# Batched matmul minus a tensor: rings of slots and one listed order of larger transfers in place of pools of four-tile buffers

## The chip, the cores and the metric

One core of a Trainium2 chip, the other cores idle. The metric is the device time of one execution in microseconds. The profile of one execution is taken beside it; its span is 1.7 to 2.2 us shorter than the time of the run. All runs told of here were in the fast state.

## The reference

```python
def setup_inputs():
    batch, m, k, n = 16, 512, 1024, 768     # all float32
    ...
def reference(x, weight, sub_value):
    return (np.matmul(x, weight) - sub_value).astype(np.float32)
```

x is 33.6 MB, the weights 3.1, sub_value and the output 25.2 each: 87.0 MB cross between HBM and SBUF.

## The kernel before

The 8192 rows are 64 tiles of 128. Of each block of 1024 rows, a partition holds eight consecutive ones, so tile j of the block is row j of each partition, and several tiles side by side are one contiguous run per partition. A tile's way: x is loaded, ScalarE casts it to f16 (`cast`), TensorE transposes it and ScalarE copies it back from PSUM (for 14 of the tiles, in pairs, VectorE transposes instead), TensorE runs 16 matmuls, VectorE subtracts sub in place (`finish`), and the result is stored. Everything is kept in program order on each engine, and the transfers are all issued from one queue, SyncE's.

```python
G = 4                       # tiles in a buffer and in a transfer
XA, SA, OA = 3, 2, 2        # groups that x and sub run ahead, and that a store comes behind
...
    x_pool = ctx.enter_context(tc.tile_pool(name="x_pool", bufs=4))
    so_pool = ctx.enter_context(tc.tile_pool(name="so_pool", bufs=7))
...
    for mi in range(HEAD, n_mt):
        g, j = divmod(mi, G)
        if j == 0 or mi == HEAD:
            if g + XA < n_g:
                load_x((g + XA) * G, G)
            if g + SA < n_g:
                load_sub((g + SA) * G, G)
            if g >= OA:
                store((g - OA) * G, G)
        ...                 # matmuls of tile mi, transposes of tile mi + 2, casts ahead
        finish(mi)
        ...
    for g in range(n_g - OA, n_g - 1):
        store(g * G, G)
    store(n_mt - G, G - 2)
    store(n_mt - 2, 1)
    store(n_mt - 1, 1)
```

## Time and profile before

| | before |
|---|---|
| time, median (all runs beside the changed kernel's) | 213.07 us (212.68 to 213.75, 4 runs) |
| span of the profiled run | 211.1 us |
| transfers, descriptors on the queue | 65, 9360 |
| share of the transfers / TensorE | 98.2% / 94% |
| last subtraction ends | 204.96 us |
| from there to the end of the span | 6.1 us |

Two resources are nearly full, so shares alone don't say which sets the end. The last two rows do: they split the end into TensorE's path and what follows it. The prediction below shows the lines. One more row matters, and the prediction didn't use it. It is from the list of transfer issues of the kernel before (count, size, median us from issue to landing), the two last stores of one tile each:

```profile
out_dram<-so_tile SPq DMA_DIRECT2D x2, 384.0 KB, 6.0
```

### The profile page before, as it was taken

What the parts mean: (1) busy time and instruction counts of PE and PEld (TensorE: products, weight loads), DVE (VectorE), ACT (ScalarE), POOL (GpSimd) and SP (SyncE); (2) the same over time, 40 slices, a digit from 0 to 9 for tenths busy, and PEclk for the clock granted to TensorE, in tenths of its full rate; (3) what the DMA queues carried; (4) which work ended last, traced back from release to release, by engine and by line L of the source; (5) the groups of instructions that cost most, each with busy time, mean ns of one, the idle gap of its engine ahead of it and who ended that gap; (6) DMA issues with size and microseconds to landing.
All of it is one profiled execution on the core that took longest, in us unless ns stands there. A gap on an engine that the chain in (4) does not pass through costs nothing.

```text
span 211.1 us, 3028 instructions
## 1 busy us (share of the span) xinstructions
PE 198.0 (94%) x1249; PEld 129.7 (61%) x1249; DVE 114.0 (54%) x186; ACT 112.7 (53%) x115; POOL 0.7 (0%) x6
## 2 busy tenths in 40 slices
PE   7899799999999999999989999997999999999960
PEld 3455567666666676676656567664656666667630
DVE  0343313152697299389519939941993993142330
ACT  3636666757852847465086555509646453556300
POOL 1000000000000000000000000000000000000000
PEclk9999999999999999999999999999999999999995
DMA  6999999999999999999999999999999999999994
GB/s 217 422 413 406 415 418 446 418 425 440 414 429 420 433 426 423 435 421 435 424 422 432 424 434 422 435 420 432 425 429 435 414 428 416 434 412 433 428 409 162
DMA packets 9374, 87.23 MB, mean 413 GB/s; under 512 B 1040, under 2 KB 1040, under 8 KB 3728
## 3 DMA queue, kind: packets, MB, share of 16 engines
q1 hardware_dynamic: 9360, 87.04, 98.2%
q8 instruction: 10, 0.16, 0.3%
q14 instruction: 4, 0.03, 0.0%
HBM read 61.87 MB, written 25.17 MB: 412 GB/s over the span
## 4 chain that ended last, share of the span: by engine, by line
DMA 49%; PE 33%; ACT 9%; DVE 3%; SPq 2%; issue 1%; ACTq 0%
DMA x_tile<-in_x_dram 49%; PE psum_o L149 28%; PE psum_t L116 5%; ACT x_tile L108 4%; ACT xt_tile L123 3%; ACT x16p_tile L105 2%; DVE xtp_tile L137 2%; DVE so_tile L160 1%; SPq L79 1%; SPq L87 1%; ACTq L105 0%
## 5 line engine op out<-in xcount | busy, mean ns | idle before, releaser
L149 PE MATMUL psum_o<-w_sb,xt_tile 128*128 128x384 f16 x800 | 145.9, 326 | 1.7 <-ACT xt_tile L123 1.7
L149 PEld LDWEIGHTS <-xt_tile 128*128 128x128 f16 x800 | 78.1, 98 | 42.0 <-ACT xt_tile L123 2.8
L160 DVE TENSOR_TENSOR so_tile<-psum_o,so_tile 128x768 f32<-128x768 f32 x64 | 60.7, 956 | 57.3 <-PE psum_o L149 34.1
L123 ACT COPY xt_tile<-psum_t 128x1024 f16<-128x1024 f16 x50 | 50.6, 1012 | 58.7 <-PE psum_t L116 58.0
L137 DVE STREAM_TRANSPOSE xtp_tile<-x16p_tile 32x256 f32<-32x256 f32 x112 | 48.8, 436 | 22.4 <-ACT x16p_tile L105 20.6
L108 ACT CAST x_tile<-x_tile 128x1024 f16<-128x1024 f32 x50 | 51.7, 1049 | 7.3 <-DMA x_tile<-in_x_dram 7.3
L116 PE MATMUL psum_t<-ident,x_tile 128*128 128x128 f32 x200 | 52.4, 274 | 2.3 <-ACT x_tile L108 1.9
L149 PE MATMUL psum_o<-w_sb,xtp_tile 128*128 128x384 f16 x224 | 42.9, 326 | 0.6 <-DVE xtp_tile L137 0.6
L116 PEld LDWEIGHTS psum_t<-ident,x_tile 128*128 128x128 f32 x200 | 27.5, 141 | 16.5 <-ACT x_tile L108 4.7
L149 PEld LDWEIGHTS <-xtp_tile 128*128 128x128 f16 x224 | 21.7, 98 | 10.9 <-DVE xtp_tile L137 1.4
L105 ACT CAST x16p_tile<-x_tile 128x1024 f16<-128x1024 f32 x14 | 14.6, 1046 | 20.5 <-DMA x_tile<-in_x_dram 20.5
L81 DVE CAST w_sb<-w_stage 128x768 f16<-128x768 f32 x8 | 4.1, 556 | 10.4 <-DMA w_stage<-in_weight_dram 10.4
L177 PE MATMUL psum_o<-idle_x,idle_w 128*128 128x512 f16 x25 | 7.7, 461 | 1.3 <-DVE idle_x L172 1.3
L177 PEld LDWEIGHTS <-idle_w 128*128 128x128 f16 x25 | 2.9, 116 | 4.5 <-issue 2.4
L108 ACT ACT_TABLE_LOAD x1 | 1.3, 1283 | 0.7 <-PEq L261 0.7
L171 DVE MEMSET idle_w<- 128x64 uint32 x1 | 0.1, 112 | 0.8 <-PEq L261 0.8
masks.py:199 POOL TENSOR_SCALAR_AFFINE_SELECT ident<-ident 128x128 f32<-128x128 f32 x1 | 0.3, 292 | 0.1
L172 DVE MEMSET idle_x<- 128x256 uint32 x1 | 0.3, 272 | 0.0
masks.py:197 POOL MEMSET ident<- 128x128 f32 x1 | 0.2, 205 | 0.3 <-POOLq L261 0.3
L261 POOL MEMSET const-uint8-127<- 128x1 uint8 x1 | 0.1, 102 | 0.0
L261 POOL MEMSET const-bfloat16-1.0<- 128x1 bf16 x1 | 0.1, 101 | 0.0
L261 POOL MEMSET const-float32-0.0<- 128x1 f32 x1 | 0.1, 98 | 0.2 <-issue 0.2
(1 smaller groups left out, 0.1 us busy)
## 6 DMA issues: line engine op xcount, KB each, us to landing
x_tile<-in_x_dram SPq DMA_DIRECT2D x13, 2048.0 KB, 30.9
out_dram<-so_tile SPq DMA_DIRECT2D x15, 1536.0 KB, 31.7
so_tile<-in_sub_value_dram SPq DMA_DIRECT2D x14, 1536.0 KB, 33.0
x_tile<-in_x_dram SPq DMA_DIRECT2D x8, 512.0 KB, 10.6
w_stage<-in_weight_dram SPq DMA_DIRECT2D x4, 768.0 KB, 8.5
x_tile<-in_x_dram SPq DMA_DIRECT2D x2, 1024.0 KB, 13.0
so_tile<-in_sub_value_dram SPq DMA_DIRECT2D x4, 384.0 KB, 11.7
so_tile<-in_sub_value_dram SPq DMA_DIRECT2D x2, 768.0 KB, 13.6
```

The source lines that it names most:

```text
L79: keep(nc.sync.dma_start(out=st, in_=w_c[c]))
L81: keep(nc.vector.tensor_copy(out=w_sb[:, c, r], in_=st[:, r]))
L87: keep(nc.sync.dma_start(out=x_t[g][:, j : j + n], in_=rows(x_s, mi, n)))
L105: keep(nc.scalar.copy(out=x16_t["pair", first][:, mi - first], in_=x_t[g][:, j]))
L108: keep(nc.scalar.copy(out=x16_t[mi], in_=x_t[g][:, j]))
L116: keep(nc.tensor.transpose(ps_t[mi].bitcast(F32)[:, c * P : (c + 1) * P], x16_t[mi].bitcast(F32)[:, c * P : (c + 1) * P], ident,))
L123: keep(nc.scalar.copy(out=xt_t[mi], in_=ps_t.pop(mi)))
L137: keep(nc.vector.transpose(xt[b * Q : (b + 1) * Q, :, a * Q : (a + 1) * Q], x16[a * Q : (a + 1) * Q, :, b * Q : (b + 1) * Q],))
L149: keep(nc.tensor.matmul(po_t[mi][:, h, :NS], xt_t[mi][:, 2 * P * c + r : 2 * P * (c + 1) : 2], w_sb[:, c, r, h * NS : (h + 1) * NS], start ...
L160: keep(nc.vector.tensor_tensor(out=o, in0=po_t.pop(mi)[:, :, :NS], in1=o, op=mybir.AluOpType.subtract))
L177: keep(nc.tensor.matmul(idle_o[:, 0], idle_w, idle_x, start=True, stop=True))
L261: nc = _bacc.Bacc("TRN2", target_bir_lowering=False, num_devices=1)
```

## The change

The pools become two rings, 16 slots for x and 32 shared by sub and the output (the weights pass through eight of these first). Transfers stand in one list, up to eight tiles each, and each is issued as soon as the program has recorded what it needs: a cast for the slot of x, a subtraction for a store, an earlier store for the slot of sub. x runs ahead early; stores wait until late.

```diff
-G = 4
-XA, SA, OA = 3, 2, 2
+NX, NSO = 16, 32
-HEAD_TRANSFERS = [('x', 0, 1), ('w', 0, 0), ('x', 1, 1), ... ('x', 3, 1), ('s', 0, 1), ('x', 4, 1), ('s', 1, 1), ... ('s', 6, 2)]
+TRANSFERS = [
+    ('x', 0, 1), ('w', 0, 1), ('x', 1, 1), ('w', 1, 1), ('x', 2, 1), ('w', 2, 1),
+    ('w', 3, 1), ('x', 3, 2), ('s', 0, 1), ('x', 5, 3), ('s', 1, 3), ('x', 8, 3),
+    ('s', 4, 4), ('x', 11, 5), ('s', 8, 8), ('x', 16, 8), ('x', 24, 3), ('s', 16, 8),
+    ('x', 27, 5), ('o', 0, 8), ('s', 24, 8), ('x', 32, 8), ('s', 32, 8), ('o', 8, 8),
+    ('x', 40, 8), ('s', 40, 8), ('x', 48, 8), ('o', 16, 8), ('o', 24, 8), ('s', 48, 8),
+    ('x', 56, 8), ('s', 56, 8), ('o', 32, 8), ('o', 40, 8), ('o', 48, 8), ('o', 56, 4),
+    ('o', 60, 2), ('o', 62, 1), ('o', 63, 1),
+]
...
+    x_ring = x_pool.tile([P, NX, K], F32)
+    so_ring = so_pool.tile([P, NSO, N], F32)
+    def issue():                # called after each cast and each finish
+        while todo:
+            kind, at, n = todo[0]
...                             # return if what it needs is not yet recorded
+            here = ring[:, at % size : at % size + n]
+            there = view[at // S][:, at % S : at % S + n]
...
-            if g + XA < n_g:
-                load_x((g + XA) * G, G)
...                             # the loads and stores of the main loop go
```

More of the change, by code (lines that the diff above doesn't have):

```diff
@@ L22 @@
 ON_DVE = frozenset(range(18, 60, 6))
-HEAD_TRANSFERS = [('x', 0, 1), ('w', 0, 0), ('x', 1, 1), ('w', 1, 0), ('x', 2, 1), ('w', 2, 0), ('w', 3, 0), ('x', 3, 1), ('s', 0, 1), ('x', 4, 1), ('s', 1, 1), ('x', 5, 1), ('s', 2, 1), ('x', 6, 1), ('s', 3, 1), ('x', 7, 1), ('x', 8, 2), ('s', 4, 2), ('x', 10, 2), ('s', 6, 2)]
+TRANSFERS = [
[7 rows of a table added]
+]
 @with_exitstack
@@ L44 @@
     n_mt = M_TOT // P
-    n_g = n_mt // G
     NS = N // 2
@@ L59 @@
     w_pool = ctx.enter_context(tc.tile_pool(name="w_pool", bufs=1))
-    x_pool = ctx.enter_context(tc.tile_pool(name="x_pool", bufs=4))
+    x_pool = ctx.enter_context(tc.tile_pool(name="x_pool", bufs=1))
     x16_pool = ctx.enter_context(tc.tile_pool(name="x16_pool", bufs=CA + 2))
@@ L64 @@
     xtp_pool = ctx.enter_context(tc.tile_pool(name="xtp_pool", bufs=2))
-    so_pool = ctx.enter_context(tc.tile_pool(name="so_pool", bufs=7))
+    so_pool = ctx.enter_context(tc.tile_pool(name="so_pool", bufs=1))
     psum_t_pool = ctx.enter_context(tc.tile_pool(name="psum_t", bufs=2, space=bass.MemoryType.PSUM))
@@ L73 @@
     w_sb = w_pool.tile([P, n_c, 2, N], F16)
-    x_t, so_t, x16_t, xt_t, ps_t, po_t = {}, {}, {}, {}, {}, {}
-    def load_w(c):
-        st = so_pool.tile([P, 2, N], F32, name="w_stage", tag="so_tile")
-        keep(nc.sync.dma_start(out=st, in_=w_c[c]))
-        for r in range(2):
-            keep(nc.vector.tensor_copy(out=w_sb[:, c, r], in_=st[:, r]))
-    def load_x(mi, n):
-        g, j = divmod(mi, G)
-        if j == 0:
-            x_t[g] = x_pool.tile([P, G, K], F32, name="x_tile")
-        keep(nc.sync.dma_start(out=x_t[g][:, j : j + n], in_=rows(x_s, mi, n)))
@@ L89, in load_sub @@
-    def load_sub(mi, n):
-        g, j = divmod(mi, G)
-        if j == 0:
-            so_t[g] = so_pool.tile([P, G, N], F32, name="so_tile")
-        keep(nc.sync.dma_start(out=so_t[g][:, j : j + n], in_=rows(sub_s, mi, n)))
-    def store(mi, n):
-        g, j = divmod(mi, G)
-        keep(nc.sync.dma_start(out=rows(out_s, mi, n), in_=so_t[g][:, j : j + n]))
+    x_ring = x_pool.tile([P, NX, K], F32)
+    so_ring = so_pool.tile([P, NSO, N], F32)
+    x16_t, xt_t, ps_t, po_t = {}, {}, {}, {}
@@ new lines @@
+    todo = list(TRANSFERS)
+    done = {"w": set(), "x": set(), "s": set(), "o": set(), "cast": set(), "finish": set()}
+    def issue():
+        while todo:
+            kind, at, n = todo[0]
+            span = set(range(at, at + n))
+            old = {t - NX if kind == "x" else t - NSO for t in span}
+            need, by = {
+                "w": (set(), "o"),
+                "x": ({t for t in old if t >= 0}, "cast"),
+                "s": ({t for t in old if t >= 0}, "o"),
+                "o": (span, "finish"),
+            }[kind]
+            if not need <= done[by]:
+                return
+            todo.pop(0)
+            done[kind] |= span
+            if kind == "w":
+                first = NSO - 2 * (n_c - at)
+                st = so_ring[:, first : first + 2]
+                keep(nc.sync.dma_start(out=st, in_=w_c[at]))
+                for r in range(2):
+                    keep(nc.vector.tensor_copy(out=w_sb[:, at, r], in_=st[:, r]))
+                continue
+            ring, size, view = {
+                "x": (x_ring, NX, x_s), "s": (so_ring, NSO, sub_s), "o": (so_ring, NSO, out_s)
+            }[kind]
+            here = ring[:, at % size : at % size + n]
+            there = view[at // S][:, at % S : at % S + n]
+            if kind == "o":
+                keep(nc.sync.dma_start(out=there, in_=here))
+            else:
+                keep(nc.sync.dma_start(out=here, in_=there))
@@ L99, in cast @@
     def cast(mi):
-        g, j = divmod(mi, G)
+        assert mi in done["x"]
+        done["cast"].add(mi)
+        x_in = x_ring[:, mi % NX]
         first = mi - mi % 2
@@ L104, in cast @@
                 x16_t["pair", mi] = x16p_pool.tile([P, 2, K], F16, name="x16p_tile")
-            keep(nc.scalar.copy(out=x16_t["pair", first][:, mi - first], in_=x_t[g][:, j]))
-            return
-        x16_t[mi] = x16_pool.tile([P, K], F16, name="x16_tile")
-        keep(nc.scalar.copy(out=x16_t[mi], in_=x_t[g][:, j]))
+            keep(nc.scalar.copy(out=x16_t["pair", first][:, mi - first], in_=x_in))
+        else:
+            x16_t[mi] = x16_pool.tile([P, K], F16, name="x16_tile")
+            keep(nc.scalar.copy(out=x16_t[mi], in_=x_in))
+        issue()
     def transposes(mi):
@@ L157, in finish @@
     def finish(mi):
-        g, j = divmod(mi, G)
-        o = so_t[g][:, j].rearrange("p (h n) -> p h n", h=2)
+        assert mi in done["s"]
+        done["finish"].add(mi)
+        o = so_ring[:, mi % NSO].rearrange("p (h n) -> p h n", h=2)
         keep(nc.vector.tensor_tensor(
@@ L162, in finish @@
         ))
-    for kind, at, n in HEAD_TRANSFERS:
-        {"w": lambda: load_w(at), "x": lambda: load_x(at, n), "s": lambda: load_sub(at, n)}[kind]()
+        issue()
+    issue()
     idle_w = const_pool.tile([P, P], F16)
@@ L218 @@
     for mi in range(HEAD, n_mt):
-        g, j = divmod(mi, G)
-        if j == 0 or mi == HEAD:
-            if g + XA < n_g:
-                load_x((g + XA) * G, G)
-            if g + SA < n_g:
-                load_sub((g + SA) * G, G)
-            if g >= OA:
-                store((g - OA) * G, G)
         t = mi + TA
@@ L241 @@
         del waiting[:PER]
-    for g in range(n_g - OA, n_g - 1):
-        store(g * G, G)
-    store(n_mt - G, G - 2)
-    store(n_mt - 2, 1)
-    store(n_mt - 1, 1)
+    assert not todo
 _INS = ['x', 'weight', 'sub_value']
```

## The prediction

> **What bounds the kernel now.** I read the page first: the DMA row and the DMA queues, then the busy shares, then the chain that ended last.
>
> ```profile
> span 211.1 us, 3028 instructions
> PE 198.0 (94%) x1249; PEld 129.7 (61%) x1249; DVE 114.0 (54%) x186; ACT 112.7 (53%) x115; POOL 0.7 (0%) x6
> PEclk9999999999999999999999999999999999999995
> DMA  6999999999999999999999999999999999999994
> ...
> q1 hardware_dynamic: 9360, 87.04, 98.2%
> ...
> DMA 49%; PE 33%; ACT 9%; DVE 3%; SPq 2%; issue 1%; ACTq 0%
> ```
>
> The transfers look like the bound: 98.2% busy over the whole span. But TensorE is at 94%, and the last things in the chain are matmuls, one subtraction and a store. So there are two near-bounds, and the question is which of them sets the end. The windows (columns: length, busy time and count of each engine, clock, DMA share, GB/s) answer that:
>
> ```profile
> 4.00:6.00 2.00, 2.00 (x9) 0.84 (x8) 0.00 (x0) 1.04 (x1) 0.00 (x0) 1.00 1.01 420
> ...
> 20.00:25.00 5.00, 3.60 (x25) 2.38 (x24) 1.20 (x2) 2.69 (x3) 0.00 (x0) 1.00 1.04 416
> ...
> 100.00:110.00 10.00, 9.24 (x59) 5.89 (x58) 3.15 (x4) 3.88 (x5) 0.00 (x0) 1.00 1.01 427
> ...
> 140.00:150.00 10.00, 8.85 (x58) 5.77 (x56) 4.12 (x8) 6.62 (x7) 0.00 (x0) 1.00 1.00 424
> ...
> 202.00:204.00 2.00, 1.97 (x13) 0.98 (x10) 0.36 (x1) 0.00 (x0) 0.00 (x0) 1.00 0.98 415
> 204.00:206.00 2.00, 0.00 (x0) 0.00 (x0) 0.96 (x1) 0.00 (x0) 0.00 (x0) 1.00 0.95 395
> 206.00:208.00 2.00, 0.00 (x0) 0.00 (x0) 0.00 (x0) 0.00 (x0) 0.00 (x0) 0.53 0.79 321
> 208.00:210.00 2.00, 0.00 (x0) 0.00 (x0) 0.00 (x0) 0.00 (x0) 0.00 (x0) 0.50 0.17 68
> ```
>
> TensorE's last matmul ends at 204.0, the last subtraction at 204.96, the last bytes move shortly after 208, and the span ends at 211.1. So the end is the later of two paths: last subtraction + 6.1 us (issue, first byte, bytes, landing), or last byte + about 2.8 us. In the kernel before both arrive together.
>
> TensorE's own floor. In the steady part a tile costs 0.651 us for each four matmuls (2.604 us a tile), and 0.109 us for each of its four transposes (0.436 more), as the chain of waits shows in pairs of 0.65 and 0.11. The main loop's first transpose comes at 22.48 us, after a stall of 1.40. From there 61 tiles are worked: 61 x 2.604 = 158.8, and 45 tiles transposed on TensorE x 0.436 = 19.6: 178.4 us, so 200.9 at best. It ends at 204.0: about 3.0 us of stalls after 22.5, which the windows place at 100 to 160 (0.76 + 0.08 + 0.23 + 1.15 + 0.31 = 2.5). Their cause is in ScalarE's timeline:
>
> ```profile
> 106.12 1.04 ACT L105 CAST x16p_tile<-x_tile 128x1024 f16<-128x1024 f32 x1 [6.91 <-DMA x_tile<-in_x_dram]
> ...
> 142.85 1.05 ACT L105 CAST x16p_tile<-x_tile 128x1024 f16<-128x1024 f32 x1 [7.30 <-DMA x_tile<-in_x_dram]
> ```
>
> These are casts for a pair of tiles that VectorE transposes. They are asked for seven tiles ahead, x has not landed, and ScalarE, which works in order, is held up.
>
> **What the Trainium skill says.** "HBM Reference", section Access: a core streaming alone reaches about 425 GB/s, bounded by its 16 DMA engines. The trace agrees: 424 to 433 in the ten-microsecond windows. "DMA: Bandwidth & Descriptors", section Measured, has 341 GB/s for 1 MB and 425 for 16 MB, single transfers on another issuing path. Here transfers of 0.4 to 0.8 MB already run at 415 to 431 between 4 and 15 us, because eight are in flight; so little is left for larger ones. The same page, section "Why a DMA increments its semaphore by 16 and not by 1", asks for one semaphore per transfer in flight. Both built programs have eight of them, and a transfer waits for the landing of the one eight before it: in the trace the store issued at 106.11 goes as the x load of 75.14, eight issues earlier, lands at 106.1.
>
> **The change part by part.** No instruction of TensorE, VectorE or ScalarE is added, removed or moved in the built program; only the transfers change: 65 issues become 39.
>
> 1. Fewer, larger transfers. Descriptors on the queue go from 65 x 144 = 9360 to 39 x 144 = 5616 (128 rows and 16 semaphore writes each). My estimate of a transfer's overhead: the head's 0.54 MB average ran at about 415 GB/s, the steady 1.7 MB average at 427. The difference, 0.068 us per MB, over 1/0.54 - 1/1.7 = 1.26 transfers per MB gives 0.054 us a transfer. 26 fewer save 1.4 us of DMA time.
>
> 2. Stores queue up behind each other at the end, so the engines stay full. The bytes after 204 us (0.79 + 0.64 + 0.14 = 1.57 MB) would take 3.7 us at 425: ends at 207.7, not 208.2; 0.5 saved. With part 1 the last byte is near 206.3, and that path ends at 206.3 + 2.8 = 209.1.
>
> 3. The head gets coarser. x3 comes with x4, x5 to x7 in one, sub 1 to 3 in one. A tile of x is 0.524 MB, of sub or out 0.393, a quarter of the weights 0.786. Summing in the listed order, and reading when that many bytes had moved from the windows:
>  - x3 and x4 are complete at 5.77 MB, moved by 16.4; landed about 17.4. Before, x3 alone landed at 15.97.
>  - x5 to x7: 7.73 MB, moved by 21.2. Landings trail the mean by some 2.2 us there (x6 before: 8.0 MB, moved by 21.9, landed 24.2). So 23.4; the cast of x5 was at 21.38 before. The main loop's first transpose moves from 22.5 to about 24.5: 2.0 us of TensorE lost.
>  - sub 1 to 3: 8.91 MB, moved at 24.0, landed 26.4. PSUM has three output buffers, so tile 4 waits until tile 1 is subtracted at 27.4, when TensorE would reach it at 26.9: 0.5 us lost.
>
> 4. Ahead of pair 18. x16 to x23 is one transfer behind sub 8 to 15: complete at 22.0 MB, moved at 54.8, landed 57.0. The cast of x18 is asked for at 52.8 (51.3 in the trace before, with the 2.5 of point 3, less the cast ahead). ScalarE stands until 57.0, the copies behind it come late by a few tenths, and VectorE's 16 transposes (four lots of 1.8 us with three subtractions of 0.98 between, 10.2 us) start near 60.9 and end near 71.1, about when tile 18 is due. I put 0.9 us on it.
>
> 5. Later pairs. Walking the list at 428 GB/s from 22.1 MB at 55 us, with 2.3 us from moved to landed: x40 to x47 (50.3 MB) lands near 123, asked for at about 123; x48 to x55 (57.6 MB) near 140, asked for near 140.5; x56 near 172, asked for at 172.6. So the 7 us waits of before go, but with no reserve; I put 0.3 us there, in place of 3.0. The queue does not run dry: its tightest place is x48 to x55, which needs tile 39's cast at 124, while the sub load ahead of it keeps the queue busy until 128.
>
> Sum on the path that sets the end: 200.9 + 2.5 + 0.9 + 0.3 = 204.6 for the last matmul, against 204.0; the span 204.6 + 0.96 + 6.1 = 211.7. The runs' time is 1.8 to 2.2 us above the span, so 213.5 to 213.9. The list looks deliberately tuned to TensorE's needs, and my landings in points 3 to 5 could each be late by half a microsecond, so I take a little off: 213.3.
>
> **The rivals.**
>
> First: the transfers set the end. For it: 98.2% busy. Then the gains of parts 1 and 2 show in full and the span is about 209.1, the time 211.2. Against it: this needs TensorE done by 202.0, which leaves only 1.1 us for all its stalls after 22.5, and the head alone takes more by my count.
>
> Second: eight-tile granularity starves the pairs. If a landing is 3 us later than I have it (for sub 48 to 55, due near 162 while tile 48 ends near 161, or x40 or x48), ScalarE stalls TensorE two or three times more, 1 to 2 us each: 214.5 to 217. For it: x lands just in time throughout. Against it: each of these waits has two tiles of buffered work behind it, and in the kernel before 7 us waits cost TensorE only about 1 us.
>
> Third: the ring blocks the queue. Held-back stores keep slots, the next sub load waits for a store's landing, and everything behind it in the one queue waits too. By the walk 5 us or more stay queued at each of these places, so I give it a small chance; a dry queue of 3 us would make 215.
>
> **Range and chances.** Over 2% faster means under 209.0, a span near 207. Even with no stall at all after 22.5, the last matmul at 200.9 gives 208.0, so this takes a better head as well: 0.02. Over 2% slower, above 217.5, needs the second and third rivals together: 0.04. Within 2%: 0.94. Eight times in ten I expect 211.2 to 215.3.
>
> **What would show it.** Right: the page has 39 issues, the steady windows 428 to 432 GB/s; the first main-loop transpose near 24.5; a wait of ScalarE for x near 53 to 57 in front of the cast for pair 18, and no 7 us waits after 100; the last matmul between 203.5 and 205.5; TensorE still in the last part of the chain. Wrong: a first transpose at 22.5 or sooner, windows after 60 us with a DMA share clearly under 1, a last matmul before 202.5 with stores still running for more than 4 us after it (first rival), or long waits for sub in front of the subtractions near 162 (second rival).

## The result, and the profile after

The changed kernel takes 211.16 us (median of 4 runs, 211.0 to 211.27) beside 213.07 before. The ratio is 0.9906, 95% interval 0.9878 to 0.9934. Ratios here are those on record for the fast runs of both kernels, so not quite the ratios of the medians. The time is within 2%, as predicted, but just under the stated range of 211.2 to 215.3. About 1.9 us were gained where the prediction, at 213.3, saw none.

The page of the changed kernel, the lines that answer to the first fence of the prediction:

```profile
span 209.4 us, 2967 instructions
...
PE 198.4 (95%) x1249; PEld 130.4 (62%) x1249; DVE 114.1 (54%) x186; ACT 112.6 (54%) x115; POOL 0.7 (0%) x6
...
q1 hardware_dynamic: 5616, 87.03, 97.7%
...
PE 68%; DMA 20%; ACT 4%; DVE 3%; SPq 1%; issue 1%
```

The descriptors are the predicted 5616. The chain of waits has gone over to TensorE. The windows of the changed kernel (columns as in the prediction):

```profile
50.00:60.00 10.00, 8.78 (x57) 5.69 (x55) 1.92 (x2) 5.75 (x7) 0.00 (x0) 1.00 1.01 430
...
100.00:110.00 10.00, 10.00 (x66) 6.54 (x65) 7.16 (x12) 5.21 (x6) 0.00 (x0) 1.00 1.01 433
...
140.00:150.00 10.00, 10.00 (x68) 6.99 (x67) 5.64 (x11) 5.72 (x7) 0.00 (x0) 1.00 1.00 429
...
202.00:204.00 2.00, 2.00 (x15) 1.21 (x13) 0.84 (x1) 0.00 (x0) 0.00 (x0) 1.00 0.83 338
204.00:206.00 2.00, 0.45 (x3) 0.06 (x1) 0.96 (x1) 0.00 (x0) 0.00 (x0) 1.00 0.60 243
206.00:208.00 2.00, 0.00 (x0) 0.00 (x0) 0.00 (x0) 0.00 (x0) 0.00 (x0) 1.00 0.56 224
```

TensorE's stalls between 100 and 160 are gone; instead it idles at 50 to 60, ahead of the pair 18 (1.2 us), for 0.3 us at 70.7, and longer in the head. And after 202 us the transfers are no longer full: the backlog has been worked off, and what is left are the last stores as they come. ScalarE's wait before pair 18 and VectorE's last subtraction in the changed kernel:

```profile
56.56 1.04 ACT L132 CAST x16p_tile<-x_ring 128x1024 f16<-128x1024 f32 x1 [3.17 <-DMA x_ring<-in_x_dram]
```

```profile
204.49 0.96 DVE L189 TENSOR_TENSOR so_ring<-psum_o,so_ring 128x768 f32<-128x768 f32 x1 [1.64 <-PE psum_o L177]
```

The last subtraction ends at 205.45, half a microsecond later than before, yet the span ends 1.7 us sooner: 3.95 us after it in place of 6.1. The last two stores, from the list of issues of the changed kernel:

```profile
out_dram<-so_ring SPq DMA_DIRECT2D x2, 384.0 KB, 3.9
```

They took 4.7 and 3.0 us (6.8 and 5.2 in the kernel before). On a queue with nothing left ahead of it such a store takes 2.3 us (runs 8, 11 and 12 below), so even the 3.0 holds about 0.7 us of standing in line.

### The profile page after: what moved, and what is told of

It is laid out like the page before. It is cut to its first block, busy times and chain, and to the rows that moved or that the text cites. A ratio compares the mean times of both kernels' runs of the same rounds, so it can differ in the third digit from the quotient of the medians.

```text
span 209.4 us, 2967 instructions
## 1 busy us (share of the span) xinstructions
PE 198.4 (95%) x1249; PEld 130.4 (62%) x1249; DVE 114.1 (54%) x186; ACT 112.6 (54%) x115; POOL 0.7 (0%) x6
## 3 DMA queue, kind: packets, MB, share of 16 engines
q1 hardware_dynamic: 5616, 87.03, 97.7%
## 4 chain that ended last, share of the span: by engine, by line
PE 68%; DMA 20%; ACT 4%; DVE 3%; SPq 1%; issue 1%
PE psum_o L177 60%; DMA x_ring<-in_x_dram 20%; PE psum_t L144 8%; ACT x_tile L135 2%; DVE xtp_tile L165 2%; ACT xt_tile L151 1%; DVE so_ring L189 1%; SPq L110 1%; SPq L122 1%; ACT x16p_tile L132 0%
## 5 line engine op out<-in xcount | busy, mean ns | idle before, releaser
L189 DVE TENSOR_TENSOR so_ring<-psum_o,so_ring 128x768 f32<-128x768 f32 x64 | 60.7, 957 | 61.2 <-PE psum_o L177 41.1
L135 ACT CAST x_tile<-x_ring 128x1024 f16<-128x1024 f32 x50 | 51.6, 1049 | 5.5 <-DMA x_ring<-in_x_dram 5.5
L132 ACT CAST x16p_tile<-x_ring 128x1024 f16<-128x1024 f32 x14 | 14.6, 1046 | 5.8 <-DMA x_ring<-in_x_dram 4.7
L205 PE MATMUL psum_o<-idle_x,idle_w 128*128 128x512 f16 x25 | 8.8, 508 | 1.3 <-DVE idle_x L200 1.3
L112 DVE CAST w_sb<-so_ring 128x768 f16<-128x768 f32 x8 | 4.1, 556 | 10.5 <-DMA so_ring<-in_weight_dram 10.5
```

Source lines behind the costliest of these rows:

```text
L112: keep(nc.vector.tensor_copy(out=w_sb[:, at, r], in_=st[:, r]))
L132: keep(nc.scalar.copy(out=x16_t["pair", first][:, mi - first], in_=x_in))
L135: keep(nc.scalar.copy(out=x16_t[mi], in_=x_in))
L189: keep(nc.vector.tensor_tensor(out=o, in0=po_t.pop(mi)[:, :, :NS], in1=o, op=mybir.AluOpType.subtract))
L205: keep(nc.tensor.matmul(idle_o[:, 0], idle_w, idle_x, start=True, stop=True))
```

## The experiments

Two theories. A: TensorE, and what it waits for, sets the end. C (the first rival of the prediction): the transfers set it, and the gain comes from fewer descriptors. Most runs make one change to the changed kernel or to another run here. Run 3 joins the edits of runs 1 and 2, run 7 starts from the kernel before, run 8 undoes the whole order after the head, and runs 9 and 10 change several things at once.

### 1. The head in single tiles

```diff
-    ('x', 3, 2), ('s', 0, 1), ('x', 5, 3), ('s', 1, 3),
+    ('x', 3, 1), ('s', 0, 1), ('x', 4, 1), ('s', 1, 1), ('x', 5, 1), ('s', 2, 1), ('x', 6, 1), ('s', 3, 1), ('x', 7, 1),
```

> The changed kernel with the kernel before's head: x3 to x7 and sub 0 to 3 one tile each. Theory A (TensorE and what it waits for set the end, but the landing of x16 to x23 at 56.6 us re-times TensorE whatever the head does): the main loop's first transpose moves from 23.8 back to about 22.5, ScalarE then waits longer before pair 18 (about 5 us in place of 3.2), and the last matmul gains at most 0.5 us: ratio to the changed kernel 0.998 to 1.000, time 210.8 to 211.3. Rival B (the coarse head alone costs TensorE 1.9 us at the end): last matmul near 202.5, time near 209.5. Rival C (the transfers set the end): no change of time and the last bytes at the same 207.9.

Measured: 212.02 us, ratio 0.9946 (0.9934 to 0.9959); worse than the changed kernel by 0.9 us (the two intervals touch at 0.9934, the single runs don't overlap), and outside all three expectations. The main loop's first transpose did move to 22.68, and the head's gain was lost to later landings, as theory A said, but most of it sooner than at pair 18: TensorE waits 0.34 us at 34.7 and 1.19 at 48.2 for subtractions that wait for sub, and then 1.4 in place of 1.1 at pair 18, whose x ScalarE gets at 56.87. The load of sub 8 to 15 lands at 47.2 here and at 47.0 in the changed kernel, so an earlier head only waits longer for it. That the time went up, theory A did not say. Five more transfers are 45 more descriptors an engine; by the size found in run 5 these are 0.3 us. The rest was not isolated; the windows between 10 and 20 us ran at 415 and 402 GB/s in place of 428 and 428.

### 2. x16 to x19 ahead

```diff
-    ('s', 8, 8), ('x', 16, 8),
+    ('s', 8, 4), ('x', 16, 4), ('s', 12, 4), ('x', 20, 4),
```

> The changed kernel with x16 to x19 moved ahead of sub 12 to 15 (sub 8-11, x16-19, sub 12-15, x20-23, four tiles each). Theory A: x16 to x19 land near 48, ScalarE no longer waits before pair 18, TensorE's idle time between 50 and 60 us (1.2 us) and between 70 and 80 (0.3) goes, last matmul near 203.0 and time 209.7 to 210.2. Rival C (the transfers set the end): time stays at 211.0 to 211.4.

Measured: 211.39 us, ratio 0.9918 (0.9903 to 0.9933), not distinguished from the changed kernel. TensorE did all that theory A promised, but the end did not move. VectorE's last subtraction and the last windows of this run:

```profile
202.52 0.96 DVE L189 TENSOR_TENSOR so_ring<-psum_o,so_ring 128x768 f32<-128x768 f32 x1 [1.64 <-PE psum_o L177]
```

```profile
202.00:204.00 2.00, 0.49 (x3) 0.10 (x1) 0.96 (x1) 0.00 (x0) 0.00 (x0) 1.00 0.92 384
204.00:206.00 2.00, 0.00 (x0) 0.00 (x0) 0.00 (x0) 0.00 (x0) 0.00 (x0) 0.65 0.84 341
206.00:208.00 2.00, 0.00 (x0) 0.00 (x0) 0.00 (x0) 0.00 (x0) 0.00 (x0) 0.50 0.27 108
```

The subtraction ends at 203.48, 2.0 us earlier, and the span at 209.6: 6.1 us behind it again. The transfers, still at 0.92 and 0.84 after 202, have their backlog to move, whether TensorE is done or not. Freeing TensorE alone is worth nothing: theory A alone falls.

### 3. Both

> Both edits: head of single tiles and x16 to x19 ahead. Theory A: TensorE gains the head's 1.9 us and the 1.5 us of pair 18, less what later landings (x40 to x47 near 122, sub 48 to 55 near 161) take back, so the last matmul lands between 201 and 203. The transfers then bound it: 87 MB at 430 GB/s from about 3 us are through near 206, so the span cannot be below about 207.5 and the time 209.0 to 210.0. If the transfers already set the end in the changed kernel (rival C), the time stays near 211.2.

Measured: 212.02 us, ratio 0.9951 (0.9938 to 0.9964): a miss, above the expected 209 to 210. The last subtraction ends at 203.68, the span at 209.9. TensorE's lead does not show, and the head's cost of run 1 does.

### 4. The same order in pieces of four

```diff
 each transfer of eight becomes two of four, each of five one of four and one of one, for example
-    ('x', 32, 8), ('s', 32, 8),
+    ('x', 32, 4), ('x', 36, 4), ('s', 32, 4), ('s', 36, 4),
```

> The changed kernel's list in the same order, but every transfer of five or eight tiles cut into pieces of four (60 issues in place of 39, so nearly as many as the 65 before). If the order gives the gain (theory O): time within 0.5 us of the changed kernel, 210.7 to 211.6, or a little better because pieces land sooner. If the size of the transfers gives it (theory S, 0.054 us per transfer as in the prediction): 21 more transfers cost 1.1 us of transfer time, steady windows back to 427 GB/s, and the time is 212 or more.

Measured: 212.58 us, ratio 0.9978 (0.9967 to 0.9989). This takes back three quarters of the gain (0.0072 of 0.0094), though the order is the changed kernel's and TensorE finishes earlier than in any run with full work: the last subtraction ends at 203.09. The tail is 7.5 us. So the size of the transfers, not their order, makes the gain; 21 transfers cost 0.0072 x 213 = 1.5 us, 0.07 each.

### 5. Same transfers, shorter rows

```diff
-            here = ring[:, at % size : at % size + n]
+            # tile t lies at slot (t % 8) * (size // 8) + (t // 8) % (size // 8)
+            a = (at % 8) * (size // 8) + (at // 8) % (size // 8)
+            here = ring[:, a : a + (n - 1) * (size // 8) + 1 : size // 8]
```

> The changed kernel with its ring slots interleaved in SBUF, so that every transfer of n tiles is made of rows of one tile (4 KB of x, 3 KB of sub and out): the same 39 transfers in the same order, but 25,600 data descriptors (1600 on each engine) in place of 4992 (312). If the overhead is one of descriptors (1.9 us between before and changed over 208 fewer data descriptors on each engine, so about 9 ns each), 1288 more cost some 11 us: time about 222. If it is one of transfers (0.07 us each, whatever their rows), the number of transfers is unchanged and the time stays within 0.7 us of 211.2.

Measured: 220.22 us, ratio 1.0326 (1.0309 to 1.0343). The number of transfers, bytes and their order are the same; only the rows are 3 and 4 KB in place of up to 24 and 32. The cost is 0.042 x 213 = 8.9 us over 1288 descriptors on each engine, 7 ns each. The middle of this run, and then of the changed kernel:

```profile
100.00:150.00 50.00, 50.00 (x325) 33.53 (x324) 35.19 (x62) 27.29 (x29) 0.00 (x0) 1.00 1.03 410
```

```profile
100.00:150.00 50.00, 50.00 (x325) 33.54 (x324) 36.21 (x64) 28.95 (x30) 0.00 (x0) 1.00 1.00 429
```

TensorE does the same work in both; only the transfer rate differs. So the overhead goes with the rows, and so with their descriptors. If each costs 7 ns whatever its length, the change's 234 fewer on each engine (9360 - 5616 over 16) are 1.6 us of its 1.9 to 2.0, and the 189 of run 4 are 1.3 of its 1.5. One thing isn't separated: in this run a transfer's tiles also lie apart in SBUF, so the 7 ns are for more rows and their spacing together.

### 6. 2.1 MB more, late

```diff
     ('o', 48, 8),
+    ('r', 48, 4),      # x48 to x51 once more into their own slots
```

> The changed kernel with one more transfer of 2.1 MB (x48 to x51 loaded again into their own slots, after their casts) queued just after the store of tiles 48 to 55; no engine's work changes and the result is right. If the transfers set the end: 2.1 MB at 430 GB/s is 4.9 us, nearly all of it on the end: span about 214.0, time 215.5 to 216.3, and TensorE's last matmul still at about 204.4. If TensorE and a fixed path after its last tile set the end: time below 212.5.

Measured: 216.05 us, ratio 1.0132 (1.0117 to 1.0148). The last subtraction stays (ends at 205.31), and the tail grows from 3.95 to 8.9 us. The expected 4.9 us are there in full.

### 7. The kernel before with 1.18 MB less, late

```diff
-                store((g - OA) * G, G)
+                store((g - OA) * G, 1 if g - OA == 13 else G)   # wrong on purpose: three tiles missing
```

> The kernel before with one of its late stores (tiles 52 to 55) cut to a quarter: 1.18 MB less to move late, no engine's work changed; three tiles of the output are missing, so the result is wrong on purpose. If the tail after the last subtraction (6.1 us in the kernel before) is backlog of the transfers: last subtraction still ends near 205.0, the tail falls to about 4 us, time 210.7 to 211.3. If the 6.1 us are a fixed latency of the last store, as the prediction took it: time stays 213.0.

Measured: 210.65 us, ratio 0.9876 (0.9862 to 0.9891), with three tiles missing from the output, as intended. The last subtraction ends at 204.91, and the tail is 4.1 us in place of 6.1. VectorE's last subtraction and the windows behind it:

```profile
203.95 0.96 DVE L160 TENSOR_TENSOR so_tile<-psum_o,so_tile 128x768 f32<-128x768 f32 x1 [1.64 <-PE psum_o L149]
```

```profile
204.00:206.00 2.00, 0.00 (x0) 0.00 (x0) 0.91 (x1) 0.00 (x0) 0.00 (x0) 1.00 0.42 171
206.00:208.00 2.00, 0.00 (x0) 0.00 (x0) 0.00 (x0) 0.00 (x0) 0.00 (x0) 0.68 0.41 161
```

The shares were 0.95 and 0.79 in the kernel before. The last store takes 3.1 us from issue to landing in place of 5.2. This decides the prediction's faulty step: at least 2.0 of the 6.1 us were backlog and not latency.

### 8. Large transfers in the old order

```diff
-    ('x', 24, 3), ('s', 16, 8), ('x', 27, 5), ('o', 0, 8), ('s', 24, 8), ('x', 32, 8), ('s', 32, 8), ('o', 8, 8), ...
+    ('s', 16, 8), ('o', 0, 8), ('x', 24, 8), ('s', 24, 8), ('o', 8, 8), ('x', 32, 8), ('s', 32, 8), ('o', 16, 8), ...
```

> The changed kernel with its large transfers, but in the steady order of the kernel before: x, sub, then the store of the group finished two groups ago, with no x ahead and no store held back (38 transfers). If size is all that counts (transfer count and bytes set the end, theory S): the time stays near 211.1. If large pieces need the order: x40 to x47 is then complete at 53.4 MB in place of 50.3, so it lands near 130 while it is asked for near 121, pairs 42 and 48 stall TensorE several us, the last matmul ends at 207 or later and the time is 213.5 to 218.

Measured: 221.32 us, ratio 1.0394 (1.0362 to 1.0425): in the direction of "large pieces need the order", but worse than the 218 given, and earlier than expected. It is not x40 but x24 to x31 that first comes too late, behind a store of eight. ScalarE's cast of this run, and TensorE's windows around it:

```profile
80.99 1.04 ACT L132 CAST x16p_tile<-x_ring 128x1024 f16<-128x1024 f32 x1 [12.66 <-DMA x_ring<-in_x_dram]
```

```profile
70.00:80.00 10.00, 6.78 (x44) 4.27 (x41) 3.59 (x5) 0.00 (x0) 0.00 (x0) 1.00 1.00 428
80.00:90.00 10.00, 7.00 (x28) 4.08 (x29) 4.95 (x10) 6.68 (x7) 0.00 (x0) 0.66 1.01 433
```

ScalarE stands 12.7 us, TensorE gets through 44 and 28 matmuls in ten microseconds in place of some 66, partly at a granted clock of 0.66, and the last subtraction comes at 216.2. So the order does not make the gain; it makes the large transfers possible.

### 9. and 10. Two attempts at something better

```diff
-    ('w', 2, 1), ('w', 3, 1), ...   ('s', 8, 8), ('x', 16, 8), ...   ('o', 56, 4), ('o', 60, 2), ('o', 62, 1), ('o', 63, 1)
+    ('w', 2, 2), ...   ('s', 8, 4), ('x', 16, 8), ('s', 12, 4), ...   ('o', 56, 6), ('o', 62, 2)
 the lines that load two quarters of the weights at once are left out here
 second attempt, on top of this:
-S = 8
+S = 16
-    ('o', 16, 8), ('o', 24, 8), ...  ('o', 32, 8), ('o', 40, 8)
+    ('o', 16, 16), ...  ('o', 32, 16)
```

> An attempt to beat both: x16 to x23 put ahead of sub 12 to 15 as one transfer (so TensorE is not held up before pair 18), the last two quarters of the weights in one transfer, the last eight tiles stored in two transfers of six and two: 37 transfers in place of 39, 16 or so descriptors an engine fewer, at about 7 ns each. If transfers and their descriptors set the end: 0.1 to 0.3 us below the changed kernel, 210.8 to 211.1; the last subtraction ends near 203.5. A gain of more than 1 us would say that TensorE set the end after all.

> The same, with sixteen consecutive rows of a partition in place of eight, so that out 16 to 31 and 32 to 47 are stored in one transfer each (35 transfers). By descriptors another 18 an engine fewer: 0.1 us below best_a. If rows 64 KB apart in HBM are slower or faster than rows 32 KB apart, this shows it as a different rate in the windows.

The first: 211.16 us, ratio 0.9924 (0.9911 to 0.9937). That is not distinguished from the changed kernel, so nothing was found that beats it. The second: 216.29 us, ratio 1.0168 (1.0151 to 1.0186), a miss by 5 us, and an instructive one. Its windows between 150 and 160, and VectorE's wait behind it:

```profile
150.00:160.00 10.00, 10.00 (x66) 6.49 (x65) 6.34 (x11) 5.07 (x6) 0.00 (x0) 1.00 0.66 253
```

```profile
165.45 0.96 DVE L191 TENSOR_TENSOR so_ring<-psum_o,so_ring 128x768 f32<-128x768 f32 x1 [8.75 <-DMA so_ring<-in_sub_value_dram]
```

The load of sub 48 to 55 needs the slots that the store of out 16 to 23 frees. Merged with out 24 to 31, that store lands only at 154.3; the load, and all that stands behind it in the one queue, waits, and the transfers run dry to 0.66. This is the prediction's third rival, which did not happen in the change as it stands. The rate was not lower elsewhere (437 GB/s between 100 and 150), so rows 64 KB apart are not the cause.

### 11. and 12. Where TensorE's own path ends

```diff
-    ('o', 48, 8),
+    ('o', 48, 2),      # wrong on purpose: six tiles missing
 once on the run of x16 to x19 ahead, once on the changed kernel itself
```

> The run with x16 to x19 ahead, with the store of tiles 48 to 55 cut to two tiles: 2.36 MB less late in the queue, so 5.5 us less for the transfers and nothing less for TensorE; six tiles of the output are missing, wrong on purpose. With the transfers out of the way the end is set by the last subtraction (203.5) and an empty queue behind it (3.95 us in the changed kernel): span 207.2 to 207.7, time 209.0 to 209.6. This is where TensorE's own path ends.

> The changed kernel with the store of tiles 48 to 55 cut to two tiles (2.36 MB, 5.5 us of transfers less; wrong on purpose). If both paths end together in the changed kernel: TensorE's last matmul stays near 204.4, the last subtraction ends at 205.4, and an empty queue behind it takes 3.3 us (as in the run of x16 to x19 ahead with the short store) to 3.95: span 208.7 to 209.4, time 210.4 to 211.2, so at most 0.7 us gained from 5.5. If the transfers alone set the end of the changed kernel: several us gained, time below 209.5.

Measured: 208.28 us (ratio 0.9786, 0.977 to 0.9803) and 210.48 us (ratio 0.9876, 0.9856 to 0.9896), both with the tiles missing, as intended. The first is somewhat below its expectation, because the tail on an empty queue is 3.3 us, not 3.95. The two last stores of the changed kernel with the tiles missing, from its list of issues:

```profile
out_dram<-so_ring SPq DMA_DIRECT2D x2, 384.0 KB, 2.3
```

The same 5.5 us of transfers, taken away, are worth about 3 us where TensorE had been freed (2.8 by the ratios, 3.1 by the medians), and at most some 0.7 us in the changed kernel (the intervals of the two ratios overlap). Taken with run 2 (TensorE 2.0 us earlier, nothing gained): in the changed kernel both paths end within about 0.7 us of each other.

All runs in one table; the tail is the span less the end of the last subtraction:

| run | transfers | descriptors an engine | last subtraction ends | span | tail |
|---|---|---|---|---|---|
| before | 65 | 585 | 204.96 | 211.1 | 6.1 |
| changed | 39 | 351 | 205.45 | 209.4 | 3.95 |
| head in single tiles | 44 | 396 | 205.75 | 209.9 | 4.2 |
| x16 to x19 ahead | 41 | 369 | 203.48 | 209.6 | 6.1 |
| both | 46 | 414 | 203.68 | 209.9 | 6.2 |
| pieces of four | 60 | 540 | 203.09 | 210.6 | 7.5 |
| short rows | 39 | 1639 | 210.09 | 218.5 | 8.4 |
| 2.1 MB more | 40 | 360 | 205.31 | 214.2 | 8.9 |
| before, 1.18 MB less | 65 | 585 | 204.91 | 209.0 | 4.1 |
| old order, large | 38 | 342 | 216.23 | 219.5 | 3.3 |
| changed, 2.36 MB less | 39 | 351 | 205.60 | 208.8 | 3.2 |
| x16 to x19 ahead, 2.36 MB less | 41 | 369 | 203.33 | 206.6 | 3.3 |
| first attempt (run 9) | 37 | 341 | 203.02 | 209.1 | 6.1 |
| second attempt (run 10) | 35 | 323 | 207.20 | 214.3 | 7.1 |

The tail is 3.2 to 3.3 us where the transfers have nothing left, and up to 8.9 where they have. About 0.9 us of it (0.8 to 1.1) follows the landing of the last store in every run. Nearly all the rest is that store's time from issue to landing: 2.3 us in the three runs with tails of 3.2 and 3.3, 3.0 in the changed kernel, 5.2 in the kernel before, 8.0 in the run with 2.1 MB more.

## Why the prediction was right or wrong

The step that failed is in the sum: "the span 204.6 + 0.96 + 6.1 = 211.7". Its first term came out right, 204.6 for the last matmul and 204.45 measured, but in part by luck: the head cost 1.9 us in place of 2.5 and the later pairs nothing in place of 0.3, while pair 18 cost 1.6 in place of 0.9. (The floor's 61 tiles also count four matmuls, 0.65 us, that come before the first transpose; still, without its waits TensorE needed 178.5 us from there, against the 178.4 of the floor.) The 6.1 was taken from the kernel before as a fixed path ("issue, first byte, bytes, landing"), though the prediction had itself counted 1.57 MB still to move after 204 us there. Of the 6.1, the last store's issue to landing took 5.2, and 2.3 is what it takes with nothing ahead of it. In the changed kernel the term measured 3.95; runs 7, 11 and 12 show 4.1, 3.3 and 3.2 when bytes are taken away, run 6 shows 8.9 when they are added. Everything above 3.2 or 3.3 is the transfers' backlog, so counting it on TensorE's path counted the transfers twice. With 3.95 the sum gives 204.6 + 0.96 + 3.95 = 209.5, beside 209.1 for the transfers' path; the span was 209.4. A check was at hand. The Trainium skill's page "DMA: Bandwidth & Descriptors", section "Anatomy of one DMA — SWDGE (gpsimd) path", gives for a single transfer about 2.0 us fixed plus bytes over 436 GB/s. For a store of 0.393 MB that is 2.9 us, an estimate from that page, for another issuing path. Measured here on an emptied queue it is 2.3, so the estimate is 0.6 too long for these stores, but far enough under 6 to warn. The 6.0 us median of the kernel before's last two was the sign that they stood in line.

- Part 1, "0.054 us a transfer", 1.4 us for 26: right in kind, a little small. Run 4 measured 0.07, and run 5 that it goes with descriptors at about 7 ns each on an engine. The change's own 1.9 us over 26 is 0.073.
- Part 2, the transfers' path at 209.1: the sum was near (209.4, and 209.6 in run 2, where TensorE is out of the way), its two halves were not. Half-microsecond windows of the kernel before still show 68 GB/s at 209.0 to 209.5, and its last packet ends at 209.8, so the span ends 1.3 us after the last byte and not 2.8; in the changed kernel the last packet ends at 208.1 and not 206.3, again 1.3 before the end. The two errors cancel. The path was discarded as the first rival, on the claim that it "needs TensorE done by 202.0". That claim was the 6.1 again: with a tail of 3.3 to 3.95 it would have read 204.2 to 204.8, and TensorE was done at 204.5.
- Part 3, the head: first transpose at 24.5 predicted, 23.78 measured; the wait for sub 1 at tile 4 0.5 predicted, 0.56 measured. The 2.0 us were 1.3, because x5 to x7 landed at 21.9 and not at 23.4.
- Part 4: x16 to x23 landed at 57.0 predicted, 56.56 measured; VectorE's transposes for the pair end at 71.1 predicted, 70.64 measured. The landings were right, but the cost was 1.6 us (1.2 at 58.6 to 59.5, where ScalarE's copies came late, and 0.3 at 70.7) in place of 0.9.
- Part 5: the long waits went, as said. TensorE has no idle time between 100 and 160. One wait of 1.5 us for x is left, at 122.2, and one of 2.4 for sub at 161.0, both at landings that the prediction had named as close.
- Second rival (starved pairs): absent in the change, shown by run 8 when the order is undone. Third rival (the ring blocks the queue): absent in the change, shown by run 10.
- Two readings: the ten-microsecond windows of the kernel before run from 419 GB/s (160 to 170), not from 424, to 433. The sentence of "HBM Reference" on about 425 GB/s stands in its section Specifications (TRN2).

What stays open: 0.3 to 0.4 us of the gain that 7 ns a descriptor does not cover, whether the tiles' spacing in SBUF has a part in these 7 ns, and most of the 0.9 us that the head in single tiles costs.

## What to carry to other kernels

When two resources are both near full, work out both end times separately, and don't take a tail measured under backlog as a latency: compare the last transfer's time from issue to landing with what the same transfer takes on an empty queue. Gains on one path are capped by the other, so test each by freeing it alone (move work earlier for one, drop bytes for the other) before tuning it. Long contiguous rows paid here, on a queue that was full for nearly the whole span, but larger pieces land later and free slots later, so the order of the transfers has to be reworked with their size.

## What the Trainium skill lacked or had wrong

- "DMA: Bandwidth & Descriptors", section Specifications, gives 512 B as the smallest transfer for line rate. On a full queue, rows of 3 and 4 KB ran at 410 GB/s and rows of 24 and 32 KB at 429, with the same transfers, bytes and order: about 7 ns for each descriptor on an engine, 8.9 us of 211 here. The page counts an overhead for each packet in cycles, in its section on small descriptors, but has no measured time for each of them on a full queue of rows this long.
- The same page's section Measured ties efficiency to the size of a transfer. Run 5 kept that size and changed only the rows, and the cost followed the rows; what a transfer costs beyond its descriptors could not be told from zero (7 ns a descriptor leave some 0.3 us of the change's 1.9).
- "HBM Reference", section Specifications (TRN2), has about 425 GB/s for a core alone; the changed kernel held 429 to 430 in each stretch of fifty microseconds between 50 and 200.
- "DMA: Bandwidth & Descriptors" fits the time of a single transfer for the gpsimd path alone. From SyncE's queue, with nothing ahead of it, a store of 0.393 MB took 2.3 us here, against 2.9 by that fit.
